# A hybrid encoder layer on one core: plain products for the first two column pairs of the FFN up projection, and grouped mLSTM numerators

## The chip, the cores and the metric

The kernel runs on one core of a Trainium2 chip. The metric is the device time of one execution in microseconds (us). A change below about 0.5% can't be told from no change here.

## The reference, cut to what matters

One encoder layer works on 1024 tokens of width 1024 in float32: a modulation vector from a condition, a normalised input, one wide input projection, four mixers (RWKV-7, mLSTM, RG-LRU, HGRN2), their gated merge and an output projection, and then a second normalisation and a convolutional FFN. The change touches three places.

```python
mod = cond @ ada_w[l] + ada_b[l]                       # 6 x 1024 values
num = (s_inter[..., None] * einsum("bhcld,bhcdv->bhclv", q, c_prev)
       + einsum("bhcls,bhcsv->bhclv", pw, v))          # mLSTM numerator, two products added
u2 = _rmsnorm(h, norm2_g[l]) * (1.0 + sc2) + sh2
z = _dwconv(u2 @ w_up, cw, cb)                         # w_up: 1024 x 5632
val, gate = split(z, 2); ffn = (val * silu(gate)) @ w_down
```

## The kernel before, in words

The layer is kept with features on the 128 partitions and tokens along the free side. Large products take float32 operands split in two parts, `hi` rounded to the matmul's type and `lo` what is left, and add three matmuls for each pair of operands: hi·hi, hi·lo, lo·hi (`mm3`, lines 123 to 127). A weight block of 4 x 128 rows by 128 columns is loaded and split by `wsplit` and `wsplit_sb` (lines 87 to 121): DMA into `w_raw` on SyncE's queue, `hi` by VectorE (line 118) or, where `wact` is set, by ScalarE (line 116), `lo` by GpSimd (line 119). There are three buffers of each. The order in which each engine issues its instructions is not written out by hand: the tile framework plans it from priorities and its own model of durations. `wsplit` raises the priority of its loads and splits, and `issue_after` keeps a matmul behind a given one.

**FFN up projection (lines 1775 to 1915).** The 44 column tiles of 128 form 22 pairs (value tile f, gate tile f + 22). Tokens come in two halves, H0 and H1. The second normalisation runs on each half in turn (`n2`, line 1740): two groups of small matmuls give a row of factors, VectorE multiplies each of eight tiles `hT` by it (line 1759), and the result is split into `uh` and `ul`. For k = 0, 2, 4, 6 ScalarE writes `uh` with the shift (line 1764) and VectorE writes `ul` (line 1765); for odd k ScalarE adds the shift in place (line 1761), ScalarE rounds (line 204) and GpSimd subtracts (line 205). Pair f = 0 is computed in plain products: 2 tiles x 2 halves x 8 blocks x 3 = 96 matmuls (`up_start`, line 1779). All others go through one step of Strassen's scheme (`strassen`, line 1826): seven products of 12 matmuls instead of eight, on sums of weight blocks (`comb`, line 1842) and sums of activations. The latter are made once, by `t_sums` (line 1795): for each of four k, four sums in `hT` (lines 1805 and 1807), four `hi` by ScalarE (line 1816) and four `lo` (line 1817), two by VectorE and two by GpSimd. The sums t1 and t3 overwrite the H1 halves of `ul` and `uh`, so their rounding waits for the last matmul that reads those.

The order around H1 is: on H0, f = 0 (48 matmuls) and two Strassen products of f = 1 (24), while `n2` of H1 runs; on H1, f = 0 (48) and one product of f = 1 (12); then, after `t_sums`, the other four products of f = 1 (48). That is 108 matmuls from the first one on H1 to the end of f = 1. Pair f = 2 is a Strassen pair like all behind it. The convolution of a pair (`up`, line 1891) takes four passes of VectorE.

**mLSTM (lines 571 to 658).** `ml_pair` works on two heads. For each head and direction, over eight chunks of 128 tokens in groups of 3, 3 and 2, two float32 matmuls a chunk add into one PSUM region: `D` against `v` over 128 rows (line 643) and `Qd` against `St` over 64 rows (line 644), alternating chunk by chunk. Two pairs x two heads x two directions make eight such units. ScalarE copies each group out (line 648). Projections and gates fill TensorE between them (`fill`).

**Modulation (`ada`, `ada_end`, lines 1372 to 1411).** In the same stage 16 steps each take 256 columns of `ada_w`: VectorE accumulates six of the eight row blocks into one tile (lines 1382 and 1384), GpSimd two into another (lines 1391 and 1395), and TensorE sums both over partitions with a column of ones: 2 x 2 matmuls of one column a step (line 1408).

Of the kernel before, what the change touches and what calls it, by code (L numbers as in the profile page):

```python
# [18 lines left out]
P = 128  # L19
# [4 lines left out]
class K:  # L24
# [78 lines left out]
        return w  # L103

    wact = False
    WB = {"raw": 3, "": 3, "raw_f": 1, "_f": 2}

    def wsplit_sb(self, raw, kt, n=P, st=""):
        nc = self.nc
        w = []  # L110
        for k0 in range(0, kt, self.CK):
            m = min(self.CK, kt - k0)
            hi = self.t(self.wpool, [P, m, n], "w_hi" + st, dt=F32R, bufs=self.WB[st])
            lo = self.t(self.wpool, [P, m, n], "w_lo" + st, dt=F32R, bufs=self.WB[st])
            if self.wact:
                nc.scalar.copy(hi, raw[:, k0:k0 + m])  # L116
            else:
                nc.vector.tensor_copy(out=hi, in_=raw[:, k0:k0 + m])  # L118
            nc.gpsimd.tensor_tensor(lo, raw[:, k0:k0 + m], hi.bitcast(F32), op=SUB)  # L119
            w += [(hi[:, i, :], lo[:, i, :]) for i in range(m)]  # L120
        return w

# [450 lines left out]
    def ml_pair(self, p, qT, kT, v, hs, wp):  # L573
# [40 lines left out]
        for hh in range(2):  # L614
# [19 lines left out]
                    nc.vector.tensor_tensor(D[d][:, 4 * i:4 * i + 4, :], D[d][:, 4 * i:4 * i + 4, :], pt, op=MUL)  # L634
            for d in range(2):
                num = self.t(wp, [P, NCK, 129], f"ml_num{d}")
                for g in range(0, NCK, 3):
                    n = min(3, NCK - g)
                    pt = self.ps([P, 512])
                    for i in range(n):  # L640
                        c = g + i
                        o = pt[:, 129 * i:129 * i + 129]
                        nc.tensor.matmul(o, lhsT=D[d][:, c, :], rhs=v[:, c, h, :], start=True, stop=False)
                        mm = nc.tensor.matmul(o, lhsT=Qd[d][r, c * P:(c + 1) * P], rhs=St[d][r, c, :],
                                              start=False, stop=True)
                    self.last_mm0 = mm
                    self.fill(mm, self.MF[1])
                    nc.scalar.copy(num[:, g:g + n, :], pt[:, :129 * n].rearrange("p (n v) -> p n v", v=129))
                dn = self.t(wp, [P, NCK], f"ml_dn{d}")
                nc.vector.scalar_tensor_tensor(dn, num[:, :, 128], -1.0, num[:, :, 128], op0=MUL, op1=MAX)  # L650
                nc.vector.tensor_tensor(dn, dn, self.mlcol["em"][:, :, 32 * d + h], op=MAX)
                nc.vector.reciprocal(dn, dn)
                rb = dn.unsqueeze(2).to_broadcast([P, NCK, P])
                if d == 0:
                    nc.vector.tensor_tensor(hs[hh], num[:, :, :P], rb, op=MUL)
                else:
                    nc.gpsimd.tensor_tensor(num[:, :, :P], num[:, :, :P], rb, op=MUL)
                    nc.vector.tensor_tensor(hs[hh], hs[hh], num[:, :, :P], op=ADD)
# [701 lines left out]


    GR = 4
    N2P = (1, 3)
    TP = (1, 3)
    SL = (1, 3)
    SP = (3,)
    SR = 6
# [4 lines left out]
    def ada(self, g0, g1, wp, G=4, bufs=2, ks=8, pend=None):  # L1372
# [3 lines left out]
        for g in range(g0, g1, G):  # L1376
# [18 lines left out]
                        nc.gpsimd.tensor_tensor(acc, acc, x, op=ADD)  # L1395
                accs.append(acc)
            if pend is None:
                self.ada_end([(g, accs)], "pa", G)
            else:
                pend.append((g, accs))  # L1400

# [58 lines left out]
    def run(self):  # L1460
# [279 lines left out]
        def n2(i):  # L1740
# [12 lines left out]
                nc.vector.tensor_scalar(dg[:, n, :], self.ident, r4[:, n:n + 1], None, op0=MUL)  # L1753
                self.n2_mm2 = nc.tensor.matmul(r[:, P * n:P * n + P], lhsT=onesP, rhs=dg[:, n, :], start=True, stop=True)

            for k in (0, 4, 1, 5, 2, 6, 3, 7):
                v = hT[k][:, sl]
                uh, ul, sh = self.uh[k][:, sl], self.ul[k][:, sl], self.mod[:, 24 + k:25 + k]
                nc.vector.scalar_tensor_tensor(v, v, self.g2s[:, k:k + 1], r, op0=MUL, op1=MUL)
                if k % 4 in self.N2P:  # L1760
                    nc.scalar.activation(v, v, AF.Identity, bias=sh)
                    self.split(v, uh, ul, "a", "p")
                else:
                    nc.scalar.activation(uh, v, AF.Identity, bias=sh)
                    nc.vector.scalar_tensor_tensor(ul, v, sh, uh.bitcast(F32), op0=ADD, op1=SUB)
# [10 lines left out]
        es = ExitStack()  # L1776
        wp = es.enter_context(tc.tile_pool(name="ffu", bufs=1, reuse_waits="tile"))
        H0, H1 = HS
        def up_start(h, zz):

            for b in range(2):
                w = self.wsplit(a["ffn_up"][0, :, P * NF * b:P * NF * b + P], 8)
                if b or h:
                    pin = [self.n2_mm2] * 2 if h == 0 else [None] * 2
                else:
                    pin = [None, self.n2_mm]
                pt = self.ps([P, 512], ("big", "pa", "big", "py")[2 * h + b])
                sl = HS[h]
                for q in range(2):
                    with self.tc.issue_after(pin[q].ins) if pin[q] is not None else ExitStack():  # L1790
                        for k in range(4 * q, 4 * q + 4):
                            self.mm3(pt, w[k][0], w[k][1], self.uh[k][:, sl], self.ul[k][:, sl], k == 0, k == 7)
                nc.scalar.copy(zz[b][:, 1 + 512 * h:513 + 512 * h], pt)

        def t_sums():
            for k in range(4):
# [20 lines left out]
                    (nc.gpsimd if i in self.TP else nc.vector).tensor_tensor(los[t], f[q], his[t].bitcast(F32), op=SUB)  # L1817

        def new_z():
            zz = [self.t(wp, [P, T + 2], f"z{b}", bufs=2 - b) for b in range(2)]  # L1820
            for z in zz:
                nc.gpsimd.memset(z[:, 0:1], 0.0)
                nc.gpsimd.memset(z[:, T + 1:T + 2], 0.0)
            return zz

        def strassen(f):

            def prep(x, y=None):

                with self.tc.high_priority(offset=self.WP):  # L1830
# [1 line left out]
                    lo = self.t(self.wpool, [P, 4, P], "w_lo", dt=F32R, bufs=3)  # L1832
                    nc.scalar.copy(hi, x)  # L1833
                    self.st_n += 1
                    (nc.gpsimd if self.st_n < 3 or self.st_n % self.SL[1] < self.SL[0] else nc.vector).tensor_tensor(  # L1835
                        lo, x, hi.bitcast(F32), op=SUB)
                return [(hi[:, i], lo[:, i]) for i in range(4)]

# [16 lines left out]
            s2 = comb(2, s1, a11, SUB)  # L1855
            s3 = comb(3, a11, a21, SUB)
            s4 = comb(4, a12, s2, SUB)
            if f == 1:
                yield
            u = lambda k, h: (self.uh[k][:, HS[h]], self.ul[k][:, HS[h]])  # L1860
            tt = lambda k, t: (BQ[k][0][t], BQ[k][1][t])

# [9 lines left out]
            lo, hi = slice(1, 513), slice(513, 1025)  # L1872
            add = lambda o, x, y: nc.vector.tensor_tensor(o, x, y, op=ADD)
            nc.scalar.copy(p1, prod(prep(a11), lambda k: u(k, 0)))
            p3 = lambda: prod(prep(s4), lambda k: u(k + 4, 1))
            if f == 1:
                add(zz[0][:, lo], p1, prod(prep(a12), lambda k: u(k + 4, 0)))
                yield
                x3 = p3()
            add(u2, p1, prod(prep(s2), lambda k: tt(k, "t2")))  # L1880
            if f > 1:
                add(zz[0][:, lo], p1, prod(prep(a12), lambda k: u(k + 4, 0)))
            add(u3, u2, prod(prep(s3), lambda k: tt(k, "t3")))
            x = prod(prep(s1), lambda k: tt(k, "t1"))
            add(zz[1][:, hi], u3, x)
            add(u2, u2, x)
            add(zz[1][:, lo], u3, prod(prep(a22), lambda k: tt(k, "t4")))
            add(zz[0][:, hi], u2, x3 if f == 1 else p3())
            yield zz

        def up(f, zz):
            for b in range(2):
# [11 lines left out]
        s1 = strassen(1)  # L1904
        next(s1)
# [6 lines left out]
        z = new_z()  # L1912
        up_start(0, z)
        with tc.issue_after(self.n2_mm2.ins):
            next(s1)
        up_start(1, z)
        t_sums()
        up(0, z)
        for f in range(1, NF):
            up(f, next(s1 if f == 1 else strassen(f)))  # L1920
        es.close()
        self.ptags = [("big", "big"), ("pa", "py"), ("pc", "pc"), ("ps", "pt")]
        wp = self.pool("ff")
# [184 lines left out]
```

## Time and profile before

| | us |
|---|---|
| median of 3 runs (2736.83 to 2750.53) | 2744.59 |
| the profiled execution | 2752.19 |
| its span from first to last instruction | 2750.4 |

The profile is of one execution. Engines are named PE (TensorE), PEld (its weight loads), DVE (VectorE), ACT (ScalarE), POOL (GpSimd) and SP (SyncE). PEclk is the granted TensorE clock: 1.00 is 2.4 GHz, 0.50 is 1.2 GHz. A float32 matmul counts as two instructions. The durations of PE's instructions overlap, so its pace is read from one start to the next.

### The profile page before, as it was taken

To read this page: it belongs to the slowest core of one execution; us is meant where nothing else is said; L and a number is where in the kernel's file an instruction comes from. 1 tells how busy PE (TensorE), PEld (TensorE's weight loads), DVE (VectorE), ACT (ScalarE), POOL (GpSimd) and SP (SyncE) were. 2 spreads that over 40 slices of the span, in tenths; PEclk is the share of its full clock that TensorE was granted. 3 is DMA by queue.
4 is the path that set the end of the run, shared out by engine and by line. 5 is a ranking of instruction groups with operands and counts; after the bars stand their busy time and mean duration, and the time that the engine had idled before them with its cause. 6 is when DMAs were issued, how large, how long until landed. Compare 5 with 4: busy or idle time off the path is not lost. (4 is left out here: it accounts for less than half of the span.)

```text
span 2750.4 us, 46997 instructions
## 1 busy us (share of the span) xinstructions
PE 2539.7 (92%) x18625; PEld 2032.3 (74%) x18625; DVE 1781.4 (65%) x2868; ACT 916.3 (33%) x1653; POOL 1178.2 (43%) x1164
## 2 busy tenths in 40 slices
PE   5999888999999999799989999999998999999998
PEld 4777666676776777587778767788776888887887
DVE  7567765676667733754553675367479998896345
ACT  4355532333333322433332232111234444342002
POOL 3654462443344315632212443367456444445332
PEclk9999998999999999999989988999999999999999
DMA  6422253444444324311111544554542222216222
GB/s 214 130 70 65 89 153 79 115 108 111 105 106 113 95 72 132 88 44 41 47 32 36 154 132 140 184 189 156 174 121 88 92 83 79 85 57 202 83 80 77
DMA packets 402117, 290.25 MB, mean 106 GB/s; under 512 B 121258, under 2 KB 364248, under 8 KB 401896
## 3 DMA queue, kind: packets, MB, share of 16 engines
q1 hardware_dynamic: 362920, 247.85, 31.1%
q10 hardware_dynamic: 38976, 39.40, 4.3%
q8 instruction: 146, 2.39, 0.4%
q14 instruction: 75, 0.61, 0.1%
HBM read 223.40 MB, written 63.77 MB: 104 GB/s over the span
## 5 line engine op out<-in xcount | busy, mean ns | idle before, releaser
L119 POOL TENSOR_TENSOR w_lo<-w_raw,w_hi 128x512 fp32r<-128x512 f32 x284 | 393.2, 1385 | 780.9 <-DVE w_hi L118 277.7
L125 PE MATMUL pbig<-uh,w_hi 128*128 128x512 f32 x1208 | 508.2, 422 | 23.4 <-ACT w_hi L116 8.5
L127 PE MATMUL pbig<-uh,w_lo 128*128 128x512 f32 x1208 | 485.3, 403 | 6.7 <-POOL w_lo L119 6.6
L126 PE MATMUL pbig<-ul,w_hi 128*128 128x512 f32 x1184 | 477.0, 403 | 0.0
L125 PEld LDWEIGHTS pbig<-uh,w_hi 128*128 128x128 f32 x1208 | 233.3, 193 | 91.0 <-ACT gt L1230 17.4
L127 PEld LDWEIGHTS pbig<-uh,w_lo 128*128 128x128 f32 x1208 | 233.4, 194 | 62.0 <-POOL w_lo L119 10.8
L126 PEld LDWEIGHTS pbig<-ul,w_hi 128*128 128x128 f32 x1184 | 229.6, 194 | 42.0 <-issue 1.3
L118 DVE CAST w_hi<-w_raw 128x512 fp32r<-128x512 f32 x224 | 134.0, 599 | 144.9 <-PE pbig L126 82.6
L127 PE MATMUL ppc<-uh,w_lo 128*128 128x512 f32 x340 | 135.6, 402 | 2.6 <-POOL w_lo L119 2.2
L125 PE MATMUL ppc<-uh,w_hi 128*128 128x512 f32 x340 | 134.5, 400 | 1.2 <-DVE w_hi L118 1.2
L126 PE MATMUL ppc<-ul,w_hi 128*128 128x512 f32 x320 | 127.8, 400 | 0.0
L125 PE MATMUL ppa<-uh,w_hi 128*128 128x512 f32 x220 | 87.2, 397 | 5.5 <-DVE w_hi L118 5.4
L127 PE MATMUL ppa<-uh,w_lo 128*128 128x512 f32 x220 | 86.9, 395 | 0.8 <-POOL w_lo L119 0.8
L127 PE MATMUL ppy<-uh,w_lo 128*128 128x512 f32 x216 | 85.3, 395 | 1.1 <-POOL w_lo L119 1.1
L125 PE MATMUL ppy<-uh,w_hi 128*128 128x512 f32 x216 | 85.8, 397 | 0.1
L1833 ACT CAST w_hi<-s 128x512 fp32r<-128x512 f32 x84 | 52.1, 620 | 97.3 <-PE ppc L126 22.4
L126 PE MATMUL ppa<-ul,w_hi 128*128 128x512 f32 x208 | 84.1, 404 | 0.0
L126 PE MATMUL ppy<-ul,w_hi 128*128 128x512 f32 x208 | 82.7, 398 | 0.0
L127 PEld LDWEIGHTS ppc<-uh,w_lo 128*128 128x128 f32 x340 | 65.8, 194 | 17.9 <-POOL w_lo L119 2.6
L125 PEld LDWEIGHTS ppc<-uh,w_hi 128*128 128x128 f32 x340 | 65.3, 192 | 16.5 <-DVE w_hi L118 2.1
L1384 DVE SCALAR_TENSOR_TENSOR ada_acc<-ada_w,sc,ada_acc 128x256 f32<-128x256 f32 x112 | 73.1, 655 | 2.0
L204 ACT CAST uh<-h_raw 128x1024 fp32r<-128x1024 f32 x22 | 23.0, 1052 | 151.9 <-PE ppc L127 123.8
(789 smaller groups left out, 6319.1 us busy)
## 6 DMA issues: line engine op xcount, KB each, us to landing
w_raw<-in_w_in_dram SPq DMA_DIRECT2D x172, 256.0 KB
ada_w<-in_ada_w_dram SPq DMA_DIRECT2D x24, 1024.0 KB
s_raw<-in_ffn_up_dram SPq DMA_DIRECT2D x84, 256.0 KB
dG<-gt ACTq DMA_DIRECT2D x64, 256.0 KB
sgt<-dG SPq DMA_DIRECT2D x32, 512.0 KB
rw_in<-dIn SPq DMA_DIRECT2D x32, 384.0 KB
w_raw<-in_ffn_down_dram SPq DMA_DIRECT2D x44, 256.0 KB
dF<-cv SPq DMA_DIRECT2D x22, 512.0 KB
```

What stands on the lines that cost most here:

```text
L118: nc.vector.tensor_copy(out=hi, in_=raw[:, k0:k0 + m])
L119: nc.gpsimd.tensor_tensor(lo, raw[:, k0:k0 + m], hi.bitcast(F32), op=SUB)
L125: nc.tensor.matmul(pt, lhsT=wh, rhs=uh, start=start, stop=False)
L126: nc.tensor.matmul(pt, lhsT=wh, rhs=ul, start=False, stop=False)
L127: nc.tensor.matmul(pt, lhsT=wl, rhs=uh, start=False, stop=stop)
L204: nc.scalar.copy(hi, src)
L1384: nc.vector.scalar_tensor_tensor(acc, w[:, k, :], self.sc[:, k:k + 1], acc, op0=MUL, op1=ADD)
L1833: nc.scalar.copy(hi, x)
```

## The change

Five edits. In the mLSTM the matmuls of a group are issued by operand: first all chunks of `D`, then all chunks of `Qd`, with one start flag for the bank. In `ada` GpSimd adds the two accumulators first, and TensorE takes the sum: two matmuls a step instead of four. `N2P` and `TP` are emptied, so that all `ul` of the second normalisation and all `lo` of `t_sums` are made by VectorE. Pairs f = 0 and f = 1 both go in plain products, in half blocks of four k, with the weights' `hi` on ScalarE and `lo` on VectorE: on H0 three tiles (72 matmuls), on H1 three (72), and the fourth on both halves (48), so that 120 matmuls lie between the first on H1 and the end of f = 1. In the first two weight splits of Strassen's scheme GpSimd is no longer preferred.

```diff
-            nc.gpsimd.tensor_tensor(lo, raw[:, k0:k0 + m], hi.bitcast(F32), op=SUB)
+            (nc.gpsimd if self.wlo == "p" else nc.vector).tensor_tensor(lo, raw[:, k0:k0 + m], hi.bitcast(F32), op=SUB)
...
-                    for i in range(n):
-                        c = g + i
-                        o = pt[:, 129 * i:129 * i + 129]
-                        nc.tensor.matmul(o, lhsT=D[d][:, c, :], rhs=v[:, c, h, :], start=True, stop=False)
-                        mm = nc.tensor.matmul(o, lhsT=Qd[d][r, c * P:(c + 1) * P], rhs=St[d][r, c, :],
-                                              start=False, stop=True)
+                    for x in range(2):
+                        for i in range(n):
+                            c, o = g + i, pt[:, 129 * i:129 * i + 129]
+                            l, rr = ((D[d][:, c, :], v[:, c, h, :]) if x == 0 else
+                                     (Qd[d][r, c * P:(c + 1) * P], St[d][r, c, :]))
+                            mm = nc.tensor.matmul(o, lhsT=l, rhs=rr, start=(x == 0 and i == 0), stop=True,
+                                                  skip_group_check=True)
...
-    N2P = (1, 3)
-    TP = (1, 3)
+    N2P = ()
+    TP = ()
...
-                self.ada_end([(g, accs)], "pa", G)
+                if ks < 8:
+                    nc.gpsimd.tensor_tensor(acc, acc, accs[0], op=ADD)
+                self.ada_end([(g, [acc])], "pa", G)
...
-            for k in (0, 4, 1, 5, 2, 6, 3, 7):
+            for k in range(8):
...
+        def up_start(f, b, hs, q, zz, pin=None):
+            c = P * (f + NF * b)
+            w = self.wsplit(a["ffn_up"][0, 512 * q:512 * q + 512, c:c + P], 4)
+            for h in hs:
+                if q == 0:
+                    upt[f, b, h] = self.ps([P, 512], UT[f, b][h])
+            with self.tc.issue_after(pin.ins) if pin is not None else ExitStack():
+                for k in range(4):
+                    for h in hs:
+                        self.mm3(upt[f, b, h], w[k][0], w[k][1], self.uh[4 * q + k][:, HS[h]], self.ul[4 * q + k][:, HS[h]],
+                                 q == 0 and k == 0, q == 1 and k == 3)
+            if q == 1:
+                for h in hs:
+                    nc.scalar.copy(zz[b][:, 1 + 512 * h:513 + 512 * h], upt[f, b, h])
...
+        self.wact, self.wlo = True, "v"
+        z = [new_z() for _ in range(2)]
+        up_start(0, 0, (0,), 0, z[0])
+        up_start(0, 0, (0,), 1, z[0], self.n2_mm)
+        for f, b in ((0, 1), (1, 0)):
+            for q in range(2):
+                up_start(f, b, (0,), q, z[f], self.n2_mm2)
+        for f in range(2):
+            for q in range(2):
+                for b in range(2):
+                    up_start(f, b, (0, 1) if f and b else (1,), q, z[f], self.n2_mm2)
         t_sums()
-        up(0, z)
-        for f in range(1, NF):
-            up(f, next(s1 if f == 1 else strassen(f)))
+        self.wact, self.wlo = False, "p"
+        for f in range(2):
+            up(f, z[f])
+        for f in range(2, NF):
+            up(f, strassen(f))
```

The tiles `z` get two buffers each, and `strassen` is an ordinary function again, with f = 1 no longer among its cases.

## Rows read from the trace of the kernel before

**Rows 1.** The page, busy time, share of the span and instructions of each engine.

```profile
PE 2539.7 (92%) x18625; PEld 2032.3 (74%) x18625; DVE 1781.4 (65%) x2868; ACT 916.3 (33%) x1653; POOL 1178.2 (43%) x1164
```

**Rows 2.** Windows: length, busy us (instructions) of PE, PEld, DVE, ACT, POOL; PEclk, DMA share, GB/s.

```profile
2050.00:2060.00 10.00, 7.47 (x20) 5.34 (x21) 10.00 (x12) 0.00 (x0) 5.37 (x4) 0.66 0.18 52
...
2070.00:2080.00 10.00, 4.43 (x16) 3.33 (x15) 10.00 (x11) 6.11 (x11) 5.57 (x5) 0.77 0.00 0
...
2100.00:2120.00 20.00, 20.00 (x90) 16.53 (x89) 19.01 (x22) 9.31 (x12) 8.96 (x8) 1.00 0.43 148
```

**Rows 3.** Waits of PE, 2028 to 2102: us in total, times, longest.

```profile
PE pps L127 <- DVE w_lo L1835: 5.6, 1, 5.6
```

**Rows 4.** Timeline of PE: start, duration, line (the last on H0; the first of f = 2).

```profile
2048.72 0.39 PE L127 MATMUL ppa<-uh,w_lo 128*128 128x512 f32 x1
...
2097.46 0.63 PE L125 MATMUL ppt<-uh,w_hi 128*128 128x512 f32 x1
...
2099.45 0.39 PE L125 MATMUL ppt<-uh,w_hi 128*128 128x512 f32 x1
2099.68 0.39 PE L126 MATMUL ppt<-ul,w_hi 128*128 128x512 f32 x1
```

**Rows 5.** Timeline of DVE and of POOL in the same stretch.

```profile
2038.25 5.36 DVE L1759 SCALAR_TENSOR_TENSOR hT<-hT,g2s,ppt 128x512 f32<-128x512 f32 x8 [2.13 <-PE ppt L1754]
...
2068.34 1.77 DVE L1817 TENSOR_TENSOR hT<-hT,t2h 128x512 fp32r<-128x512 f32 x1
2070.04 0.68 DVE L1805 TENSOR_TENSOR hT<-hT 128x512 f32<-128x512 f32 x1
2070.64 0.68 DVE L1817 TENSOR_TENSOR hT<-hT,ul 128x512 fp32r<-128x512 f32 x1
...
2067.82 1.74 POOL L1835 TENSOR_TENSOR w_lo<-s,w_hi 128x512 fp32r<-128x512 f32 x1
```

**Rows 6.** A window in the mLSTM stage, columns as in Rows 2.

```profile
1620.00:1640.00 20.00, 16.57 (x82) 12.69 (x81) 14.84 (x24) 12.89 (x27) 9.41 (x7) 0.62 0.30 105
```

**Rows 7.** Groups of PE, 1540 to 1748: busy us, mean ns, idle before.

```profile
L605 PE MATMUL ppt<-ml_v,ml_wk 128*64 128x129 f32 x44 | 4.3, 331 | 6.4 <-DVE ml_wk L594 3.4 <-DVE ml_S L610 3.0
```

**Rows 8.** Timeline of PE, numerators: one group of three, and one at the lower clock.

```profile
1655.36 0.39 PE L643 MATMUL ppt<-ml_v,ml_D 128*128 128x129 f32 x2
1655.67 0.49 PE L644 MATMUL ppt<-ml_S,ml_q 64*128 64x129 f32 x2
...
1657.76 0.50 PE L125 MATMUL pbig<-uh,w_hi 128*128 128x512 f32 x1
...
1612.39 0.80 PE L643 MATMUL pps<-ml_v,ml_D 128*128 128x129 f32 x2
1613.12 0.80 PE L644 MATMUL pps<-ml_S,ml_q 64*128 64x129 f32 x2
```

**Rows 9.** Timeline of PE, float32 matmuls of one shape in a row, and what follows them.

```profile
2037.16 1.05 PE L1754 MATMUL ppt<-n_ss,onesP 128*128 128x128 f32 x8
2037.96 0.48 PE L125 MATMUL ppa<-uh,w_hi 128*128 128x512 f32 x1
...
1564.77 1.16 PE L631 MATMUL pps<-ml_qT,ml_kT 64*128 64x128 f32 x8
1565.86 0.50 PE L125 MATMUL ppc<-uh,w_hi 128*128 128x512 f32 x1
```

**Rows 10.** Modulation: timeline of PE, groups of POOL, timeline of DVE.

```profile
1649.23 0.95 PE L1408 MATMUL ppa<-ones,ada_acc 128*128 128x1 f32 x8
1650.11 0.37 PE L631 MATMUL ppt<-ml_qT,ml_kT 64*128 64x128 f32 x1
...
L1395 POOL TENSOR_TENSOR ada_acc<-ada_acc,ada_w 128x256 f32<-128x256 f32 x16 | 12.4, 778 | 1.1
...
1624.79 0.35 DVE L1382 TENSOR_SCALAR ada_acc<-ada_w,sc 128x256 f32<-128x256 f32 x1
...
1634.43 0.48 DVE L1384 SCALAR_TENSOR_TENSOR ada_acc<-ada_w,sc,ada_acc 128x256 f32<-128x256 f32 x1
```

More of the change, by code (lines that the diff above doesn't have):

```diff
@@ L105 @@
     wact = False
+    wlo = "p"
     WB = {"raw": 3, "": 3, "raw_f": 1, "_f": 2}
@@ L1778, in run @@
         H0, H1 = HS
[L1779 to L1793, printed above, removed]
+        def up_start(f, b, hs, q, zz, pin=None):
[12 more added lines that the diff above has]
+                    nc.scalar.copy(zz[b][:, 1 + 512 * h:513 + 512 * h], upt[f, b, h])
         def t_sums():
@@ L1819, in new_z @@
         def new_z():
-            zz = [self.t(wp, [P, T + 2], f"z{b}", bufs=2 - b) for b in range(2)]
+            zz = [self.t(wp, [P, T + 2], f"z{b}", bufs=2) for b in range(2)]
             for z in zz:
@@ L1834, in prep @@
                     self.st_n += 1
-                    (nc.gpsimd if self.st_n < 3 or self.st_n % self.SL[1] < self.SL[0] else nc.vector).tensor_tensor(
+                    (nc.gpsimd if self.st_n % self.SL[1] < self.SL[0] else nc.vector).tensor_tensor(
                         lo, x, hi.bitcast(F32), op=SUB)
@@ L1857, in strassen @@
             s4 = comb(4, a12, s2, SUB)
-            if f == 1:
-                yield
             u = lambda k, h: (self.uh[k][:, HS[h]], self.ul[k][:, HS[h]])
@@ L1874, in strassen @@
             nc.scalar.copy(p1, prod(prep(a11), lambda k: u(k, 0)))
[L1875 to L1879, printed above, removed]
             add(u2, p1, prod(prep(s2), lambda k: tt(k, "t2")))
-            if f > 1:
-                add(zz[0][:, lo], p1, prod(prep(a12), lambda k: u(k + 4, 0)))
+            add(zz[0][:, lo], p1, prod(prep(a12), lambda k: u(k + 4, 0)))
             add(u3, u2, prod(prep(s3), lambda k: tt(k, "t3")))
@@ L1887, in strassen @@
             add(zz[1][:, lo], u3, prod(prep(a22), lambda k: tt(k, "t4")))
-            add(zz[0][:, hi], u2, x3 if f == 1 else p3())
-            yield zz
+            add(zz[0][:, hi], u2, prod(prep(s4), lambda k: u(k + 4, 1)))
+            return zz
         def up(f, zz):
@@ L1903, in run @@
         self.st_n = self.st_t = 0
-        s1 = strassen(1)
-        next(s1)
         BQ = {}
@@ L1910, in run @@
             BQ[k] = his, {}
[L1912 to L1916, printed above, removed]
-        t_sums()
-        up(0, z)
-        for f in range(1, NF):
-            up(f, next(s1 if f == 1 else strassen(f)))
+        upt = {}
+        UT = {(0, 0): ("big", "big"), (0, 1): ("pa", "py"), (1, 0): ("pc", "pc"), (1, 1): ("ps", "pt")}
+        self.wact, self.wlo = True, "v"
[9 more added lines that the diff above has]
+                    up_start(f, b, (0, 1) if f and b else (1,), q, z[f], self.n2_mm2)
+        t_sums()
+        self.wact, self.wlo = False, "p"
[3 more added lines that the diff above has]
+            up(f, strassen(f))
         es.close()
```

## The prediction

> **What bounds the kernel now.** I read the page first: PE is busy in 92% of the span [rows 1], so a change pays where it takes work off PE or ends one of PE's waits. The windows then show where PE is not busy, and the change has its largest part in one such place, the start of the FFN up projection. Between 2050 and 2100 us PE is short of work and its granted clock falls to about half at times, while DVE is busy without a gap; from 2100 on PE is full again at 1.00 [rows 2]. The waits of PE in that stretch say what comes last: the low part of a weight block made by DVE, 5.6 us at once in the longest wait [rows 3]. The timeline gives its length: the last matmul on H0 starts at 2048.72, the first of f = 2 at 2097.46, and the pace of 0.23 us is back at 2099.45 [rows 4].
>
> DVE is late because of the company it keeps. The same subtraction of 128 x 512 takes 0.68 us alone and 1.77 us while POOL runs a two-operand operation, which takes 1.74 us itself [rows 5]. That is the row on which the FFN part of the argument hangs.
>
> The second place is the mLSTM stage. There PE is nearly always busy in the record; the largest idle time I found ahead of one line is 6.4 us [rows 7]. But a busy PE is not a fast one: its clock stood at 0.62 between 1620 and 1640 [rows 6], and the numerators run slowly even at the full clock [rows 8]. So work taken off PE there should shorten the stage.
>
> **Numerators.** Of a group of three chunks the six matmuls take 1657.76 - 1655.36 = 2.40 us: the first 0.31, each of the five others (2.40 - 0.31) / 5 = 0.42 [rows 8]. Matmuls of one shape in a row go faster. With 128 rows, eight instructions (four float32 matmuls) start within 0.80 us, so 0.20 each; with 64 rows within 1.09 us, so 0.27 each [rows 9]. Grouped, three chunks need 0.31 + 2 x 0.20 for the 128-row ones and 0.42 + 2 x 0.27 for the 64-row ones, 1.67 us, 0.73 less. Two chunks go from 0.31 + 3 x 0.42 = 1.57 to 0.31 + 0.20 + 0.42 + 0.27 = 1.20, 0.37 less. A unit of 3, 3 and 2 saves 1.83 us, the eight units 14.6 us. At the lower clock an alternating matmul takes 0.73 us [rows 8], so there a group may save more; I leave that for the range. No row shows a run of this very shape in this place; the bounds are nothing (the pace belongs to the operands, not to the alternation) and 14.6 us plus what the clock gives back.
>
> TensorE: Matmul & The Clock Gate, a page of the Trainium skill, says under "LDWEIGHTS (loading the stationary operand)" that a load takes as long for 32 rows as for 128, since only columns count. By that rule alone the row count would be no reason for a slower pace, and this term would be zero.
>
> **Modulation.** Sixteen steps lose two matmuls each, that is 64 instructions. Eight of them take 0.88 us [rows 10], so 64 x 0.11 = 7.0 us of PE. POOL gets 16 additions of 0.78 us [rows 10], 12.5 us over some 200 us. No DMA and no queue of SP is touched. What it adds is a wait: the addition needs DVE's accumulator, and behind it on POOL stand weight low parts, masks of `D` and the next step. DVE's six operations can be spread out: one step ran from 1624.79 to 1634.43 [rows 10]. I take this wait as covered by the projections that fill PE; uncovered, it is the rival that ends slower.
>
> **The mLSTM stage in sum.** 14.6 + 7.0 = 21.6 us off PE. A part will turn into waits that were not visible before, on the chain from `D` through ScalarE's exponentials, and PE waits a little even now [rows 7]. I count 0.8 of it, 17.3 us: a judgement from the near-absence of idle time.
>
> **FFN, what PE has to do.** From 2048.72 + 0.23 = 2048.95 to 2097.46 are 48.5 us, and from there to 2099.45 five matmuls at the low clock cost 1.99 instead of 5 x 0.23 = 1.15 us, another 0.8 [rows 4]. At the full pace the 120 matmuls of the new order need 27.6 us, with twelve matmuls (2.8 us) more than the 108 before. So 48.5 + 0.8 - 27.6 = 21.7 us are to be had if PE never waits. On H0 the work is the same, 72 matmuls.
>
> **FFN, whether DVE keeps up.** Now DVE has all of it: 16 passes of `n2` (0.67 us each by the eight that take 5.36), 16 sums and 16 low parts of `t_sums` at 0.60 (from one start to the next, 2070.64 - 2070.04), and of the 14 weight low parts some 11 after 2038, at 0.60 [rows 5]. That is 10.7 + 19.2 + 6.6 = 36.5 us: from 2038.25 to 2074.8. PE would come to f = 2 at 2048.95 + 27.6 = 2076.6. POOL is left with memsets, one sum and the first preparations of f = 2 and the product of `up`, so most operations should take 0.68. The weight parts carry a raised priority and each set serves 12 matmuls, 2.8 us, against 0.6 us of DVE and about as much of ScalarE, with three buffers. What removes the cover is DVE being held by an in-order wait, above all for the roundings of t1 and t3, which wait for the last matmul on the first four H1 tiles: 36 matmuls before the end, 8 us, with 8 low parts (4.8 us) to make. This fits, but leaves DVE without slack, and the two convolutions pile up behind it. Weight loads rise from 8 + 4 to 14 blocks of 256 KB, all on SP's queue; at 120 matmuls DMA has 8 of them to bring in 27.6 us, about 76 GB/s, while a row shows 148 in use [rows 2]. I leave 3.7 us for waits that stay: 18 us gained. The bounds are 21.7 and, if DVE sets the pace as before, about -2.8 (the twelve matmuls more).
>
> The normalisation of H0 runs beside the output projection; POOL loses four subtractions, DVE gains four. I put it at zero, within 2 us either way, by the same contention [rows 5]. The memsets and the second buffers of `z` cost nothing on a path.
>
> **Sum.** 17.3 + 18 = 35.3 us from the profiled execution's 2752.2 gives 2716.9. That execution is 7.6 us above the median of the runs shown, so for a median I forecast 2744.6 - 35 = 2710 us.
>
> **Rivals.** *Grouping brings nothing*: as by the rule above, only 0.8 x 7.0 = 5.6 us of the first term stays, 35.3 - 11.7 = 23.6, so 2721 us. Against it speak the uniform runs [rows 9]. 0.15.
>
> *DVE sets the pace of the up projection*: the low parts queue behind `t_sums`, PE stalls as before in another place, the clock falls again, and the FFN gives 0 to 8 us. 35.3 - 18 = 17.3 leaves 2719 to 2727. For it: DVE's 36.5 us against 38.4 us to the end of f = 1. Against it: contention gone. 0.15.
>
> *Slower: POOL is held by the new addition*: place, the modulation steps; price, the hold of POOL times 16, if it reaches PE through weight low parts and masks. With 3 us a step, a third of the spread that one chain shows [rows 10], 48 us are lost against 35 gained: 2757 us. It decides from 35.3 / 16 = 2.2 us a step on. Against it: PE has other work in the queue. 0.08.
>
> *The change does little*: the planner's new order moves stalls elsewhere, and the clock of the mLSTM stage is as low as before, about 2740 us. 0.10.
>
> **How the numbers follow.** The forecast has 0.52. Half a per cent is 13.7 us and about what a measurement of this kernel can tell, so faster means below 2731: the forecast, the first rival and most of the second (0.09), 0.76. The rest of the second and the fourth are the same, 0.16; slower 0.08. The low end is all of 21.6 and 21.7 with some 8 us of clock given back in the mLSTM stage (half of the 20 us window at 0.62 [rows 6], where an alternating matmul takes 0.73 instead of 0.42): 51 us, 2693. The high end takes in both faster rivals, with a margin of 7 us: 2734.
>
> **What would show it.** In the changed profile PE should be full at clock 1.00 from the last matmul on H0 to the first of f = 2, in about 28 us, and DVE's low parts there should take 0.68 us. A numerator group of three should take about 1.7 us, and the modulation's matmuls should number 64 instructions there. I am wrong if PE waits for low parts of weights between the halves, if a group still takes 2.4 us, or if POOL's additions show long idle times before them and PE waits for POOL's tiles behind.

## The result and the profile after

The changed kernel took 2710.59 us (median of 4 runs, 2707.24 to 2715.04) against 2740.71 us for the kernel before (median of 4, 2733.70 to 2750.53): 0.9889, 95% interval 0.9860 to 0.9918. Run again with three of the experiments it took 2705.84 us against 2746.70, 0.9869 (0.9845 to 0.9894). These ratios, here and below, are the record's; they are not the quotients of the two medians and can differ a little from them. By the medians the change is 30 and 41 us faster, by the ratios 30 and 36; forecast were 35 us and a time of 2710.

The profiled execution of the changed kernel is the shortest of its four (2707.24 us, span 2705.4), that of before (2752.19) lies above all four of its own. The 45 us between them are more than the change is worth; some 8 to 13 of them belong to the mLSTM stage of that one execution of before, as the table of stages below shows.

The page of the changed kernel, engines; against [rows 1] PE has 38 us less to do, POOL 30:

```profile
PE 2501.7 (92%) x18573; PEld 2010.5 (74%) x18573; DVE 1768.4 (65%) x2878; ACT 919.5 (34%) x1656; POOL 1148.6 (42%) x1150
```

The start of the up projection in its windows, columns as in [rows 2]:

```profile
2010.00:2020.00 10.00, 8.75 (x39) 6.88 (x37) 10.00 (x15) 7.27 (x12) 2.31 (x1) 1.00 0.55 158
2020.00:2030.00 10.00, 8.32 (x34) 6.23 (x34) 10.00 (x17) 2.30 (x4) 0.00 (x0) 1.00 0.38 106
2030.00:2040.00 10.00, 9.90 (x43) 8.19 (x44) 10.00 (x16) 8.28 (x15) 0.00 (x0) 1.00 0.38 107
2040.00:2050.00 10.00, 10.00 (x46) 8.26 (x45) 10.00 (x14) 9.88 (x17) 0.27 (x4) 1.00 0.26 77
```

Where the clock was at 0.66 and 0.77 in [rows 2], it is 1.00 throughout. DVE still has no gap, but POOL beside it is nearly empty, and PE is full from 2030 to 2050. The four longest waits of PE from 1985 to 2110, against the 5.6 us of [rows 3]:

```profile
PE ppc L128 <- DVE w_lo L120: 2.1, 1, 2.1
PE pps L128 <- DVE w_lo L1841: 1.8, 1, 1.8
PE ppc L128 <- POOL w_lo L1841: 0.9, 1, 0.9
PE pbig L128 <- DVE w_lo L120: 0.6, 1, 0.6
```

The timeline of PE, last matmul on H0 alone and first behind the two plain pairs' last, which answer to [rows 4]:

```profile
2023.06 0.39 PE L128 MATMUL ppc<-uh,w_lo 128*128 128x512 f32 x1
...
2051.36 0.39 PE L128 MATMUL ppt<-uh,w_lo 128*128 128x512 f32 x1
2051.58 0.39 PE L126 MATMUL ppa<-t2h,w_hi 128*128 128x512 f32 x1
```

From 2023.06 + 0.23 to 2051.58 are 28.3 us, where the kernel before needed 48.5. (Two matmuls of f = 2 start before the end of it, at 2046.60, and four of H1 before 2023.)

The numerators in its timeline of PE, one group of three at the full clock and one at the lower one, against [rows 8]:

```profile
1561.87 0.83 PE L648 MATMUL ppt<-ml_v,ml_D 128*128 128x129 f32 x6
1562.63 0.93 PE L648 MATMUL ppt<-ml_S,ml_q 64*128 64x129 f32 x6
1563.50 0.60 PE L1414 MATMUL ppa<-ones,ada_acc 128*128 128x1 f32 x4
...
1590.74 1.63 PE L648 MATMUL ppt<-ml_v,ml_D 128*128 128x129 f32 x6 [2.66 <-issue]
1592.30 1.66 PE L648 MATMUL ppt<-ml_S,ml_q 64*128 64x129 f32 x6
1593.89 0.58 PE L648 MATMUL pps<-ml_v,ml_D 128*128 128x129 f32 x1
```

1563.50 - 1561.87 = 1.63 us instead of 2.40. At the lower clock it is 1593.89 - 1590.74 = 3.15. The groups of the modulation and of the state matmuls over its mLSTM stage (1532.8 to 1718):

```profile
L1403 POOL TENSOR_TENSOR ada_acc<-ada_acc,ada_acc 128x256 f32<-128x256 f32 x16 | 15.1, 946 | 5.7 <-DVE ada_acc L1388 3.8 <-DVE ml_dn L656 0.7 <-DVE mod L1417 0.4
...
L1414 PEld LDWEIGHTS ppa<-ones,ada_acc 128*128 128x128 f32 x64 | 9.5, 198 | 5.6 <-POOL ada_acc L1403 4.1 <-issue 0.4
...
L1414 PE MATMUL ppa<-ones,ada_acc 128*128 128x1 f32 x64 | 9.1, 245 | 3.6 <-DVE hn_ss L483 3.6
...
L606 PE MATMUL ppt<-ml_v,ml_wk 128*64 128x129 f32 x56 | 5.0, 313 | 8.2 <-DVE ml_wk L595 6.0 <-DVE ml_S L611 2.2
```

64 instructions on the column of ones, as forecast. POOL's addition takes 0.95 us and not 0.78; PE waited once for one that mattered (4.1 us at the weight load; the matmul's own record puts 3.6 us down to `hn_ss`, the other operation that ended then). The wait for `ml_wk` that was 3.4 us in [rows 7] is 6.0.

### The profile page after: what moved, and what is told of

Same layout as the page of the kernel before. It is cut to its first block, busy times and chain, and to the rows that moved or that the text cites. A ratio compares the mean times of both kernels' runs of the same rounds, so it can differ in the third digit from the quotient of the medians.

```text
span 2705.4 us, 46888 instructions
## 1 busy us (share of the span) xinstructions
PE 2501.7 (92%) x18573; PEld 2010.5 (74%) x18573; DVE 1768.4 (65%) x2878; ACT 919.5 (34%) x1656; POOL 1148.6 (42%) x1150
## 4 chain that ended last, share of the span: by engine, by line
PE 53%; DVE 20%; issue 5%; DMA 3%; ACT 3%; POOL 2%; SPq 1%; ACTq 0%; DVEq 0%; POOLq 0%
PE pbig L126 8%; PE pbig L128 7%; PE pbig L127 7%; DVE rw_pr L1000 3%; PE ppc L128 2%; PE ppc L126 2%; PE ppc L127 2%; DVE s L1848 2%; PE ppy L126 1%; PE ppy L127 1%; PE ppy L128 1%; PE ppa L126 1%; PE ppa L127 1%; PE ppa L128 1%; DVE w_lo L1841 1%
## 5 line engine op out<-in xcount | busy, mean ns | idle before, releaser
L120 POOL TENSOR_TENSOR w_lo<-w_raw,w_hi 128x512 fp32r<-128x512 f32 x276 | 383.5, 1390 | 757.9 <-DVE w_hi L119 269.7
L126 PE MATMUL pbig<-uh,w_hi 128*128 128x512 f32 x1200 | 501.6, 419 | 20.4 <-ACT w_hi L117 8.5
L128 PE MATMUL pbig<-uh,w_lo 128*128 128x512 f32 x1200 | 479.1, 401 | 4.8 <-POOL w_lo L120 4.1
L117 ACT CAST w_hi<-w_raw 128x512 fp32r<-128x512 f32 x74 | 45.7, 618 | 112.3 <-PE pbig L127 52.0
```

What stands on the lines that cost most here:

```text
L120: (nc.gpsimd if self.wlo == "p" else nc.vector).tensor_tensor(lo, raw[:, k0:k0 + m], hi.bitcast(F32), op=SUB)
L126: nc.tensor.matmul(pt, lhsT=wh, rhs=uh, start=start, stop=False)
L128: nc.tensor.matmul(pt, lhsT=wl, rhs=uh, start=False, stop=stop)
```

## The experiments

Every run left one profile, and four points of PE's timeline cut each into stages: the first state matmul on `ml_wk` (mLSTM begins), the first matmul of the merge on `yh`, the start of the last one-column matmul of `n2` on H1 (the first of its two groups of small matmuls), and the end of the span. This table has, for each, the mLSTM stage (from the first to the second point) with its mean clock, the numerators in it (from the first matmul of each group to the next matmul behind it, summed over the stage), and the tail (from the third point to the end).

| run | numerators | modulation | mLSTM us | clock | numerators us | tail us |
|---|---|---|---|---|---|---|
| the kernel before | alternating | old | 213.0 | 0.88 | 59.7 | 716.2 |
| e0_before | alternating | old | 199.9 | 0.93 | 54.0 | 714.2 |
| e3_ffn_only | alternating | old | 203.6 | 0.92 | 53.7 | 701.8 |
| e6_pool_company | alternating | old | 209.1 | 0.88 | 61.0 | 710.0 |
| e2_ada_only | alternating | new | 202.3 | 0.90 | 60.5 | 717.8 |
| e4_no_group | alternating | new | 202.2 | 0.91 | 60.1 | 700.2 |
| e9_alternate_other | alternating | new | 207.0 | 0.89 | 60.5 | 701.8 |
| e1_group_only | grouped | old | 184.1 | 0.96 | 36.5 | 714.2 |
| e10_no_ada | grouped | old | 186.5 | 0.96 | 36.5 | 699.1 |
| the changed kernel | grouped | new | 185.2 | 0.93 | 43.2 | 700.2 |
| e8_after | grouped | new | 187.3 | 0.90 | 44.2 | 702.0 |
| e11_sums_gpsimd | grouped | new | 189.7 | 0.90 | 43.6 | 706.6 |
| e5_low_gpsimd | grouped | new | 181.4 | 0.95 | 36.5 | 702.7 |
| e7_ktm_early | grouped | new | 180.8 | 0.95 | 36.5 | 700.3 |

Two things are seen at once. The stage of the mLSTM spreads by 13 us among kernels with the same code in it (199.9 to 213.0), and its clock with it, so a single pair of profiles settles nothing there. And yet no alternating run is below 199.9 and no grouped one above 189.7.

### The parts alone

**e0_before**: the kernel before, unchanged.

> The kernel before once more, for a second profile of it. If the time that the changed kernel gained in the mLSTM stage of the first pair of profiles (28 us) is the change's, this profile shows the same stage length of about 213 us as the first; if the first profile of before was slow there by chance of the clock, the stage is 10 us or more shorter here.

2745.67 us, 0.9991 (0.9971 to 1.0012). The mLSTM stage took 199.9 us, 13 less than in the first profile, at a clock of 0.93 instead of 0.88. So the second branch holds: the first profile of before was slow there, with the same code.

**e1_group_only**: the kernel before with the grouped numerators.

```diff
-                    for i in range(n):
...
+                    for x in range(2):
+                        for i in range(n):
...
```

> The kernel before, with the mLSTM numerators grouped by operand and nothing else. Theory (alternating row counts is what is slow): a group of three takes about 1.65 us instead of 2.40 at the full clock, 14.6 us of TensorE go, and 10 to 15 us of the time. Rival (the pace belongs to the operands): a group still takes 2.4 us and the time stays within 3 us. Second rival (the lower clock in this stage is what costs): a group is faster, and the time falls by over 18 us because the clock stays up.

2724.15 us against 2748.76, 0.9912 (0.9892 to 0.9932), 24 us. A group of three takes 1.62 us, so the first rival falls; the time falls by more than the theory's 10 to 15 us and lands where the second rival had it, and the stage's clock is indeed high, 0.96. The stage falls to 184.1 us.

**e2_ada_only**: the kernel before with the modulation's addition on POOL.

```diff
-                self.ada_end([(g, accs)], "pa", G)
+                if ks < 8:
+                    nc.gpsimd.tensor_tensor(acc, acc, accs[0], op=ADD)
+                self.ada_end([(g, [acc])], "pa", G)
```

> The kernel before, with GpSimd adding the two accumulators of the modulation and half of its matmuls gone, and nothing else. Theory: 64 matmul instructions of 0.11 us go, 4 to 7 us of the time. Rival (the addition holds GpSimd, and TensorE waits for it or for what stands behind it): the additions show idle time before them, TensorE waits for them, and the time stays within 3 us or rises.

2741.61 us, 0.9977 (0.9960 to 0.9994): 6 us, at the edge of what can be told. Its mLSTM stage, 202.3 us, is not shorter than that of the copy of before.

**e3_ffn_only**: the kernel before with `N2P` and `TP` empty and the new start of the up projection.

```diff
-    N2P = (1, 3)
-    TP = (1, 3)
+    N2P = ()
+    TP = ()
...
+        self.wact, self.wlo = True, "v"
...
```

> The kernel before, with the whole FFN part of the change (plain products for the first two pairs, low parts there on VectorE, the second normalisation and the sums of activations without GpSimd), and nothing of the mLSTM stage. Theory: TensorE is at the full clock from H0 to the third pair, and 15 to 20 us go. Rival (VectorE still sets the pace there): 0 to 8 us.

2727.88 us, 0.9922 (0.9901 to 0.9942), 21 us, a little more than the theory's 15 to 20. The tail loses 12 to 16 us, and the time from the first one-column matmul of `n2` on H0 to the last on H1 1.4 (47.5 to 46.1).

In sum the parts give 52 us, the whole gave 30 and 41. The next runs set the whole beside two kernels with one part taken out.

### The whole, and one part taken out

**e8_after**: the changed kernel, unchanged.

> The changed kernel again, for comparison with the three below on one chip. It should give 2710 us within 4 and 0.986 to 0.992 of the kernel before. The three parts alone took off 24.2 (grouping), 6.3 (modulation) and 21.4 us (FFN), 52 in sum, against some 30 to 38 for the whole; if the single parts were rightly measured, this run stays at about 0.989 and the parts overlap.

2705.84 us (above), a little below the 2706 to 2714 expected; the ratio, 0.9869, lies in its range.

**e4_no_group**: the changed kernel with alternating numerators.

> The changed kernel with the numerators alternating again, so modulation and FFN are left. Theory that the parts add: losing the grouping costs what it gave alone, 16 to 24 us, so 2727 to 2735. Rival, that the parts overlap (the grouping meets another wait once the modulation is changed): the loss is 8 us or less, 2711 to 2719. In the stage of mLSTM the time from its first state matmul to the first matmul of the merge should go from 185 us to 200 by the first theory, to 193 or less by the second.

2721.44 us, 0.9920 (0.9896 to 0.9943): 15.6 us lost by the medians, 14 by the ratios. The time itself lies between the two ranges, which were reckoned from 2711 and not from 2705.84; the loss is just short of the 16 to 24 us of "the parts add" and well over the rival's 8, and the stage, 202.2 us, decides for the first. So grouping is worth some 15 us within the whole and 24 alone, and with intervals of 5 to 7 us on either side of each ratio these two can't be told apart.

**e10_no_ada**: the changed kernel with the old modulation.

> The changed kernel with the old modulation (no addition on GpSimd, twice the matmuls on the column of ones). By the stage lengths the modulation part gave nothing in its own stage (202.3 us against 199.9 in the copy of before), so my theory is no change, 2706 to 2714. By its single run, which took 6.3 us off, it would be 2716 to 2717. A third, that the wait of TensorE for the addition (3.6 us seen once in the changed kernel, with the tile of the FFN and merge work behind it) is a loss: 2703 to 2706.

2708.37 us, 0.9863 (0.9842 to 0.9885). By the medians it is 2.5 us slower than e8_after's 2705.84, by the ratios 1.6 us faster, and the intervals overlap almost wholly: no gain can be shown for this part. Each part looks larger alone than inside the whole; whether the parts overlap or the single runs came out high by chance is not shown.

### Why a group is faster

**e9_alternate_other**: the changed kernel with the two kinds in turn, on other PSUM columns each time.

```diff
-                    for x in range(2):
-                        for i in range(n):
-                            c, o = g + i, pt[:, 129 * i:129 * i + 129]
...
+                    for j, i in enumerate((0, 1, 2, 0, 1, 2) if n == 3 else (0, 1, 1, 0)):
+                        x = j % 2
+                        c, o = g + i, pt[:, 129 * i:129 * i + 129]
...
```

> The changed kernel with the numerators alternating between 128-row and 64-row weights again, but never two in succession into the same PSUM columns in a group of three (chunk 0, 1, 2, 0, 1, 2 with the kinds in turn). Two theories of why a group of three takes 1.63 us instead of 2.40. That the change of rows between one matmul and the next costs it: the group takes 2.4 us again and the time is that of the run without grouping, 2718 to 2725. Rival, that it is the second matmul adding into the columns that the first has just written: the group takes 1.6 to 1.7 us and the time stays at 2703 to 2712.

2727.85 us, 0.9916 (0.9893 to 0.9938): 3 us over the range of the first theory, with the ratio of e4_no_group (0.9920). Its timeline of PE:

```profile
1562.75 0.38 PE L648 MATMUL ppt<-ml_v,ml_D 128*128 128x129 f32 x2
1563.07 0.49 PE L648 MATMUL ppt<-ml_S,ml_q 64*128 64x129 f32 x2
1563.48 0.49 PE L648 MATMUL ppt<-ml_v,ml_D 128*128 128x129 f32 x2
1563.90 0.49 PE L648 MATMUL ppt<-ml_S,ml_q 64*128 64x129 f32 x2
1564.32 0.49 PE L648 MATMUL ppt<-ml_v,ml_D 128*128 128x129 f32 x2
1564.73 0.49 PE L648 MATMUL ppt<-ml_S,ml_q 64*128 64x129 f32 x2
1565.15 0.61 PE L1414 MATMUL ppa<-ones,ada_acc 128*128 128x1 f32 x4
```

1565.15 - 1562.75 = 2.40 us, the old pace to the hundredth, although in a group of three no two neighbours share PSUM columns and the start flag stands as in the grouped form. It is the turn from one kind to the other that costs about 0.2 us each time: (2.40 - 1.62) us for four turns more. Whether it is the number of rows or which rows they are wasn't told apart.

### What the FFN part owes to which edit

**e6_pool_company**: the kernel before with `N2P` and `TP` empty and nothing else.

> The kernel before with one thing changed: the sums, low parts and shifts that stood on GpSimd ahead of the up projection (half of the columns' pairs) go to VectorE; no second plain tile pair, no other part. It splits the FFN part, which alone took off 21 us and shortened the stretch from n2's last part to the end by 15. Theory that the plain products do it (TensorE has 38 us of products while VectorE makes the sums, so it no longer waits): this run keeps the waits of TensorE for the sums and gives 2740 to 2752. Rival, that GpSimd's company does it (VectorE's 128x512 operations fall from 1.77 to 0.68 us once GpSimd is idle, so the sums are ready sooner): 8 to 20 us faster, 2727 to 2738, and the second half-rate stretch of the clock in the up projection shrinks or goes.

2741.78 us, 0.9984 (0.9968 to 1.0000). By the time the theory of plain products holds; but the tail did lose some 5 us (710.0), and the long wait for one low part is gone. It is replaced by small ones (PE's waits, 2016 to 2092):

```profile
PE pps L126 <- DVE hT L1817: 3.1, 3, 1.3
PE pbig L127 <- POOL w_lo L119: 2.0, 2, 1.0
PE pbig L125 <- DVE w_hi L118: 1.6, 1, 1.6
PE ppc L127 <- DVE w_lo L1835: 1.5, 1, 1.5
```

PE now waits for the low parts of the sums themselves (`hT`, line 1817): on H1 the 48 matmuls of f = 0 and one product of f = 1 are all that it has to do until they are made.

**e11_sums_gpsimd**: the changed kernel with `N2P` and `TP` as before.

```diff
-    N2P = ()
-    TP = ()
+    N2P = (1, 3)
+    TP = (1, 3)
```

> The changed kernel with the second and fourth pair of shifts and low parts of n2 and of the sums on GpSimd again, as before; the plain products stay, their low parts on VectorE. It asks within the whole what the run with only this part asked of the kernel before, where n2's last part to the end went from 714 to 716 us to 710. Theory that the cover by plain products is what counts and VectorE's sums are hidden behind TensorE's 38 us of products: the time from n2's last part to the last matmul of the second plain tile stays at 47 us within 2, and the time at 2704 to 2714. Rival, that GpSimd's company makes VectorE the bound (eight low parts and sums at 1.7 us instead of 0.7, and low parts of the weights late): the stretch takes 50 to 56 us, with waits of TensorE for w_lo from VectorE of over 5 us in sum, and the time is 2712 to 2722.

2715.32 us, 0.9879 (0.9853 to 0.9905). The tail is 706.6 us, 6 more than the mean of the changed ones, and both of the rival's marks are there: the stretch from the third point to the end of the plain products takes 50.4 us (2009.4 to 2059.84, against 46.4 and 46.8 in the changed kernel and e8), and PE waits 5.6 us at once for a low part from DVE. It is as long as the wait of [rows 3], but in another place: on H0, in the third tile. The timeline of POOL, DVE and PE shows how:

```profile
2020.70 6.76 POOL L206 TENSOR_TENSOR ul<-hT,uh 128x512 fp32r<-128x512 f32 x4
...
2021.21 3.47 DVE L1811 TENSOR_TENSOR hT<-hT 128x512 f32<-128x512 f32 x2
...
2024.60 1.75 DVE L1771 SCALAR_TENSOR_TENSOR ul<-hT,mod,uh 128x512 fp32r<-128x512 f32 x1
2026.27 1.74 DVE L120 TENSOR_TENSOR w_lo<-w_raw,w_hi 128x512 fp32r<-128x512 f32 x1
2027.93 0.68 DVE L1848 TENSOR_TENSOR s<-s_raw,s_raw 128x512 f32<-128x512 f32 x1
2028.06 0.79 PE L128 MATMUL ppc<-uh,w_lo 128*128 128x512 f32 x1 [5.58 <-DVE w_lo L120]
```

While POOL makes four low parts of `n2`, DVE's operations take 1.74 us; the one behind them takes 0.68. The weight's low part, for which PE waits, stands behind three such operations.

With the tails of the four combinations the two edits can be weighed. The tail is 715.6 us on average without either (four runs, 714.2 to 717.8), 710.0 with `N2P` and `TP` emptied alone, 706.6 with plain products alone, 700.8 with both (seven runs, 699.1 to 702.0; e5 left out). Emptying `N2P` and `TP` is worth 5.6 or 5.8 us, the plain products 9.0 or 9.2: they add, as far as one profile each of e6 and e11 can tell. Two limits: POOL keeps its low parts of weights and the product of `up`, so this is not the price of all of its company (in e6 it is still busy for 26.8 of the 60 us from 2034 on); and the new start brings more than plain products, since in the same edit `n2` takes the tiles in the order k = 0 to 7.

**e5_low_gpsimd**: the changed kernel with `wlo` kept at "p", so that the 14 low parts of the plain products are POOL's.

> The changed kernel with the low parts of the plain products on GpSimd again; there are 14 of them. Theory that it is GpSimd's company that slows VectorE (operations of 128x512 took 1.77 us beside it and 0.68 alone, GpSimd's own 1.74): VectorE loses 14 x 0.7 us of its own work but its other operations slow by up to 1.09 us each, so its chain of sums in the up projection becomes longer than TensorE's products (36.5 + 5 against 38.4 us) and TensorE waits for low parts of 1.7 us: 4 to 12 us slower, 2714 to 2722, with waits of TensorE for w_lo from GpSimd and VectorE's 128x512 operations at 1.5 to 1.8 us. Rival, that TensorE paces the stretch wherever the low parts are made: 2708 to 2712, and the time from n2's last part to the last matmul of the second plain tile stays at 47 us.

2709.01 us, 0.9870 (0.9848 to 0.9892): the rival holds. The company is there in DVE's groups (line 1813 with `mod` alone takes 1261 ns; in e8_after it takes 744), yet the stretch ends no later, at 2049.22, 44.3 us behind the third point. This placing of the low parts changes nothing that can be told.

### A try at the wait that is left

**e7_ktm_early**: the changed kernel with the transposes of k moved behind its projection.

```diff
-        ktm = self.t(wp, [P, NCK, P], "ml_ktm")
...
+        ktm = self.ktm[p]
...
                 col(2 + p, lambda h, sl, pt: nc.scalar.copy(kk[p][:, sl], pt))
+                ktm = self.ktm[p] = self.t(wp, [P, NT, P], "ml_ktm")
...
```

> The changed kernel with the transposes of k of a head pair, and their copies, moved from the start of that pair's work to just behind k's projection. In the changed kernel TensorE waits 6.0 us for ml_wk at the start of the second pair, whose transposes wait for the first pair's numerators, and whose copies stand behind exponentials on ScalarE. Theory that this wait is the next thing on the path of mLSTM: it goes, and the stage falls from 185 to 187 us to 180 or less, 2700 to 2706 in all. Rival, that VectorE's other work or the decay matrices are late next: the stage stays within 3 us, 2704 to 2712. A loss is possible if ScalarE's copies now delay the first pair's: up to 4 us.

2711.56 us, 0.9857 (0.9832 to 0.9882), the same as the changed kernel. The stage took 180.8 us, but so it did (181.4) in e5_low_gpsimd, whose mLSTM code is that of the changed kernel. The wait for `ml_wk` is still there, 6.4 us, and DVE's timeline (with ScalarE's copy) says why:

```profile
1606.98 0.57 ACT L1623 COPY ml_ktm<-pps 128x512 f32<-128x512 f32 x1
...
1607.53 2.91 DVE L1383 SCALAR_TENSOR_TENSOR ada_acc<-ada_w,sc,ada_acc 128x256 f32<-128x256 f32 x2
...
1610.36 1.74 DVE L590 TENSOR_TENSOR ml_wk<-ml_ktm,mlc_w 128x1024 f32<-128x1024 f32 x1
```

The transposes still ran behind the first pair's last numerators, and once the copy was there DVE first made two steps of the modulation. So the edit didn't take the wait away, and what the stage would gain without it stays open. No version was found that beats the changed kernel.

## Why the prediction was right

**The sum.** 35.3 us were forecast, 30 and 41 measured. That the first measurement, 2710.59 us, falls on the forecast 2710 is in part luck: the base of 2744.6 was 4 us above the median of four, and the gain 5 us short. The two terms of the sum hold, but inside the first the two parts are wrongly weighed, one too low and one too high.

**Numerators: mechanism and size of a group right.** 1.62 to 1.63 us for three chunks at the full clock (1.67 forecast) and 1.18 for two (1.20). With sixteen and eight of them that is 16 x (2.40 - 1.62) + 8 x (1.57 - 1.18) = 15.6 us, where 14.6 stood. The factor of 0.8 laid on it for waits to come, which made 11.7 of it, took off too much: taking the grouping away cost 15.6 us, putting it in alone gave 24, and the mLSTM stage is 20.3 us shorter on average (185.0 against 205.3, seven runs each). The waits did come. Two windows over the stage, of e4_no_group and of the changed kernel, which differ in the grouping alone (columns as in [rows 2]):

```profile
1533.10:1735.30 202.20, 188.76 (x920) 144.92 (x919) 125.45 (x239) 55.47 (x121) 103.15 (x99) 0.91 0.46 143
1532.80:1718.00 185.20, 169.16 (x920) 136.94 (x919) 128.76 (x239) 55.53 (x118) 103.15 (x98) 0.93 0.50 154
```

PE's idle time is 202.20 - 188.76 = 13.4 us in the one and 16.0 in the other, and over the seven profiles of either kind 11.6 and 16.5 us on average, 5 us more. But the clock gave back more than that. By the lengths and mean clocks of the table, with the two levels 1.00 and 0.50, the stage spent some 40 us at the lower level with alternating numerators and some 24 with grouped ones: part of the alternating groups fell into half-rate stretches, where a group took 4.2 to 4.4 us against some 3.2 for a grouped one, and the numerators' sum went from 54 to 61 us to between 36.5 and 44. The prediction had left this to the range. Why the clock fell less was not tested.

**The rival that grouping brings nothing** falls by e1_group_only, e4_no_group and e9_alternate_other. TensorE: Matmul & The Clock Gate, the page of the Trainium skill, says under "LDWEIGHTS (loading the stationary operand)" that a load's time goes by columns and not by rows. The changed trace agrees for the single load: over its mLSTM stage the loads of line 648 take 226 and 216 ns on average with 128 rows and 221 and 213 with 64. The rival was wrong to conclude from it that the order can't matter; the price lies in the change between the two kinds, 0.42 us a matmul in turn against 0.20 to 0.27 in a run, which e9 shows and of which that rule doesn't speak. Another page of the Trainium skill does, and the prediction had not weighed it: TensorEngine Tiling (Array Packing) says under "Key Properties" that changing the tiling mode drains TensorE. The shapes in the trace, 128*128 and 64*128, are two such modes, and the trace agrees with its 2.40 us in turn and 1.63 in runs; that it is the draining and nothing else was not tried.

**Modulation: the work went, the time hardly.** 64 instructions fell away and PE's busy time for them from 16.3 or 17.0 us to 9.1, as forecast (7.0). The 5.6 us counted for it are not seen in the runs: 2.5 us by the medians (and none by the ratios) against e10_no_ada, 2.6 in the stage's mean with alternating numerators, 0.4 with grouped ones, all below the spread; the 6 us of e2_ada_only appear in no stage. With alternating numerators the work seems to have turned into idle time of PE, 14.4 us of the stage on average with the new modulation against 9.5 with the old. With grouped ones the table shows another possible reason. Where the grouped stage kept its clock the new modulation made it 181 us, the old one 184 and 186; but in three of five profiles with the new one the clock fell for a while, the numerators took 44 instead of 36.5 us, and the stage was at 185 to 190. Where such a stretch began PE had stood idle (2.66 us ahead of 1590.74 in the changed kernel, 2.5 and 2.4 us at the same place in e8 and e11); in the two profiles whose clock held there, e5 and e7, the gap was 1.5 and 1.4 us, and with the old modulation there was none over 1 us. That less work of PE brings this about was not tested, and two profiles of the other kind are few.

**The slower rival, POOL held by the addition,** had its place right: POOL waited 3.8 us for DVE's accumulator over the whole stage, and PE once for the sum, 4.1 us. Its point of decision was 2.2 us a step; what came was (15.1 + 5.7) / 16 = 1.3 us of POOL, nearly all hidden.

**The FFN part: 18 us forecast, 16 measured** (14.8 in the tail, 715.6 to 700.8, and 1.4 in `n2`). The step from H0 to f = 2 was nearly exact: 28.3 us at clock 1.00, about 28 forecast, DVE's 14 low parts of weights at 0.69 us each. Two small things took their part of the 3.7 us left for waits. One low part came late on H0 (2.1 us), a place that the prediction had called unchanged; with the 0.6 us on H1 it is the sign of being wrong that the prediction named, but small. And some 2 us were given back behind: from the first matmul of f = 2's second product to the end it took 653.8 and 655.2 us (the changed kernel and e8), and from f = 2's first 652.9 and 651.4 before (with e0). In the first 59 us or so of these stretches PE waited 4.2 and 3.9 us for low parts of weights, against 1.1 and 2.4 before. That the convolutions hold DVE up there was forecast; that they are the cause is argued and not shown. The chain "contention makes DVE late" holds, and e11 shows it as directly as can be, but it is worth 6 of the 16 us; 9 come from the new start, that is from PE having plain products to do meanwhile, which the prediction never separated.

**Rival two, DVE paces the stretch**, did not come, but the sum that was set against it was wrong. From the first pass of `n2` on H1 to the last low part of `t_sums` 36.5 us were counted. DVE's timeline in the changed kernel has these ends:

```profile
2009.41 5.35 DVE L1765 SCALAR_TENSOR_TENSOR hT<-hT,g2s,ppt 128x512 f32<-128x512 f32 x8
...
2060.99 1.78 DVE L1823 TENSOR_TENSOR hT<-hT,t4h 128x512 fp32r<-128x512 f32 x1
```

That is 53.4 us, about as long as in the kernel before (2038.25 to 2090.69). Left out were seven passes of the convolutions, 11.9 us, and six sums and low parts of the next pair's weights, 4 us. PE came to f = 2 11 us before this end, and its first products there found most of their operands ready. So DVE did not become free in time, as the prediction had it; PE had other work long enough. In e5, too, where POOL's company slows DVE, PE reached the end of the plain products no later.

**`n2` of H0 at zero**: 47.5 to 46.1 us between the halves, a gain of 1.4, within the 2 us stated; e6, which empties `N2P` and `TP` and nothing else, has it too.

## What to carry to other kernels

Order float32 matmuls on 128 and on 64 rows in runs of one kind rather than in turn: time a pair of neighbours of either order from one start to the next, multiply by the number of turns, and set the granted clock beside the waits before taking a share off, for here both moved, and in opposite directions. When two engines slow each other, emptying the one and giving TensorE something to do meanwhile are two remedies, to be priced apart. And where stages of unchanged code spread by 13 us between profiles, judge a part of 5 us by several profiles, not by one pair.

## What was unexpected of the hardware

The turn between 128-row and 64-row weights costs about 0.2 us whatever PSUM columns they write. And how far POOL can hold DVE back differs from case to case: the convolution's pass over 1024 columns took 1.29 us alone in the changed kernel, and 3.43 us beside POOL's product, 2.1 us more, against 1.1 us more (1.77 for 0.68) in the short case of [rows 5] (timeline of DVE and POOL):

```profile
2045.20 1.29 DVE L1896 SCALAR_TENSOR_TENSOR cv<-z,colsC,cv 128x1024 f32<-128x1024 f32 x1
...
2050.57 4.79 POOL L1899 TENSOR_TENSOR cv<-cv,cv 128x1024 f32<-128x1024 f32 x1 [3.82 <-ACT cv L1898]
...
2053.01 3.43 DVE L1896 SCALAR_TENSOR_TENSOR cv<-z,colsC,cv 128x1024 f32<-128x1024 f32 x1
```

The pass ended at 2053.01 + 3.43 = 2056.44, 1.08 us behind POOL's product (2050.57 + 4.79 = 2055.36): nearly its whole length alone, so by these times it had waited and not shared. The 4.79 us are not all POOL's work either: four operations of DVE that began between 2050.61 and 2052.41, inside POOL's record, took 0.70 us each, as those just before it did. That one of the two waits for the other is what the Trainium skill says, on its page SBUF — State Buffer under "SBUF: two separate sides": the ports that VectorE and GpSimd have in common are locked for a whole instruction.
